# Gate and up projections by seven block products for eight (one Strassen level) in an eight-core FFN and mixer kernel

## The chip, the cores and the metric

The kernel runs on all 8 cores of one Trainium2 chip (two dies: cores 0 to 3 and 4 to 7). Each core does the same work on its own 2192 tokens, with no traffic between cores. The metric is the device time of the slowest core in microseconds (us).

The same program took clearly longer in some of its executions, and in these some cores were granted a lower TensorE clock. Two numbers are given for most runs: the time of the fast runs, and the span on *clean* cores, those whose clock records hold no *reduced stretch*. This is a stretch in which the granted clock is down although TensorE is busy throughout (0.82 from 2278 to 2438 us in the run with x in fp16, core 5, by the view of stretches). In runs without a trace clean cores are picked by their mean clock. Spans are compared with spans: 2501 to 2502 us for the kernel before.

## The reference, cut to what matters

Two layers, each `x += 0.5*SwiGLU1(rms(x)); x += Mix(rms(x)); x += 0.5*SwiGLU2(rms(x))`. Width 1024, hidden width 2816 = 22 blocks of 128.

```python
def rmsnorm(x, g):
    xf = x.astype(jnp.float32)
    y = xf * lax.rsqrt(jnp.mean(xf * xf, axis=-1, keepdims=True) + EPS)
    return (y * g.astype(jnp.float32)).astype(x.dtype)

def swiglu(x, w_gu, w_down):
    gate, up = jnp.split(x @ w_gu, 2, axis=-1)
    return (jax.nn.silu(gate) * up) @ w_down
# ... mixer (RG-LRU and gated linear attention), states, final norm: unchanged by the change
```

## The kernel before

Everything is transposed: channels on partitions, tokens along columns. The activations `x` stay in SBUF as fp32 (70 KB per partition). The FFN runs in four calls, each in two halves of the tokens; a half has three tiles of 272 or 384 tokens, and beside it another half's mixer runs as independent work for the same engines. The kernel contains a list scheduler: it fixes, before anything runs, the order of the instructions of each engine, from a table of durations and a list `PLAN` of one rule per 25 us. So where an instruction is not ready its engine waits at it: after the change TensorE once stood for 7.0 us before a normed tile (`xn` L497 in the list of waits below). TensorE's results go to PSUM, eight banks in this program; a *hand-over* below means that the program lets TensorE write a bank again only when another engine has read it.

```python
TILES = [(0, 272), (272, 384), (656, 384), (1040, 384), (1424, 384), (1808, 384)]
HALVES = [[0, 1, 2], [3, 4, 5]]
NGU, NDN, NPG = 6, 5, 6        # slots: gate/up weights, down weights, pages of mixer weights
NF, NB = 10, 7                 # fp32 and bf16 buffers of the mixers
xn = sb("xn", [128, 3, KC, NMAX], F16)          # normed x of three tiles
# ... for a block j of 128 hidden channels and one tile (K = 1024 = 8 matmuls each):
P.op("pe", [mm(G, w.ap[:, kc*128:(kc+1)*128], xn[:, sl, kc, o0:o0+n], n, kc == 0, kc == KC-1) for kc in range(KC)], ...)
P.op("pe", [mm(U, w.ap[:, 1024+kc*128:1024+(kc+1)*128], xn[:, sl, kc, o0:o0+n], n, ...) for kc in range(KC)], ...)
act(sg[:, b, :n], lambda: bk(G)[:, :n], AF.Silu, ...)                        # ScalarE
tt(hb[:, hs_, jj, :n], lambda: bk(U)[:, :n], sg[:, b, :n], ALU.mult, ...)    # VectorE
# ... down projection of a group of j, for 8 blocks mc of output channels:
stt(x[:, mc, s:s+n], lambda: bk(v)[:, :n], 0.5, x[:, mc, s:s+n], ALU.mult, ALU.add, ...)   # VectorE: x += 0.5*psum
```

## Time and profile before

The median of the 3 fast runs was 2504.52 us (2504.2 to 2505.18); a fourth run was slow, 2987.9 us. The first lines come from the page of the profile: busy time by engine, four rows of the strip (40 slices, tenths busy; `PEclk` is the granted clock), the chain of work that ended last, and the four groups of the FFN (busy us, mean ns | idle before, and what ended it).

```profile
PE 2475.8 (99%) x16678; PEld 1543.5 (62%) x16678; DVE 1521.1 (61%) x3196; ACT 1327.3 (53%) x2560; POOL 625.4 (25%) x990
...
PE   7999999999999999999999999999999999999998
DVE  5545765657766568543644467665676666776346
ACT  3322678686767586311311149686848686753115
PEclk9999999999999999999999999999999999999999
...
PE 94%; ACT 3%; DVE 1%; DMA 1%; issue 0%; POOL 0%; DVEq 0%; ACTq 0%; POOLq 0%
...
L483 PE MATMUL ps<-xn,rgu 128*128 128x384 f16 (+2 forms) x8176 | 1317.3, 317 | 1.4 <-ACT sg L464 1.0
...
L470 DVE SCALAR_TENSOR_TENSOR x<-ps,x 128x384 f32<-128x384 f32 (+3 forms) x1192 | 599.8, 527 | 221.6 <-PE ps L483 190.0
L464 ACT ACTIVATE sg<-ps 128x384 f32<-128x384 f32 (+3 forms) x535 | 247.6, 470 | 833.8 <-PE ps L483 682.0
...
L476 DVE TENSOR_TENSOR hb<-ps,sg 128x384 f16<-128x384 f32 (+3 forms) x535 | 278.1, 528 | 413.7 <-PE ps L483 366.9
```

TensorE hardly waits; VectorE and ScalarE wait for it. The same from the other side is the list of TensorE's waits (what it waited for, total us, times, longest), some 20 us in all; these are its largest:

```profile
PE ps L483 <- DVE sqf L476: 9.8, 6, 7.7
PE ps L483 <- ACT sqf L464: 4.5, 4, 2.4
PE ps L483 <- ACT Bb L464: 1.7, 5, 0.5
```

`sqf` are squares for a norm. And by stretches (columns: window, then busy us and instruction counts of PE, weight loads, DVE, ACT, POOL; the last three numbers are clock, DMA share, GB/s): the first is beside a mixer, the second is FFN alone.

```profile
400.00:600.00 200.00, 199.87 (x1306) 117.12 (x1304) 125.07 (x246) 144.56 (x264) 47.16 (x78) 1.00 0.66 100
1100.00:1300.00 200.00, 200.00 (x1318) 128.77 (x1316) 100.67 (x200) 38.15 (x71) 26.91 (x45) 1.00 0.44 74
```

### The profile page before, as it was taken

Reading aid. Unit: us, or ns where it says so; the run is one execution under the profiler, and the core shown is the slowest. Engines: PE = TensorE matmul, PEld = TensorE weight load, DVE = VectorE, ACT = ScalarE, POOL = GpSimd, SP = SyncE. Lnnn points to the kernel's source line nnn. Section 1 sums busy time; section 2 is a strip of 40 time slices with the busy share of each in tenths; the row PEclk is TensorE's granted clock in tenths of the full one; section 3 lists DMA queues with packets and bytes.
Section 4 is the critical chain, followed back from the end, with each engine's and each line's share of the span. In section 5 each row is a group of like instructions: output and inputs, shape, how many; then the busy total and the mean of one; then the engine's idle time right before and its main releaser. Section 6 shows DMA issues by size and latency. Waiting matters only on the chain.

```text
span 2502.3 us, 47184 instructions; the slowest of 8 cores (2501.0 to 2502.3 us)
## 1 busy us (share of the span) xinstructions
PE 2475.8 (99%) x16678; PEld 1543.5 (62%) x16678; DVE 1521.1 (61%) x3196; ACT 1327.3 (53%) x2560; POOL 625.4 (25%) x990
## 2 busy tenths in 40 slices
PE   7999999999999999999999999999999999999998
PEld 4666665555666666666666666655566666666666
DVE  5545765657766568543644467665676666776346
ACT  3322678686767586311311149686848686753115
POOL 2222232313221314310201042313132314142102
PEclk9999999999999999999999999999999999999999
DMA  9656677666776779544444357676767667986412
GB/s 185 121 106 99 109 119 108 104 103 94 107 112 106 120 129 157 94 77 71 78 72 68 52 83 109 95 120 88 123 98 113 108 105 105 165 138 140 68 26 77
DMA packets 118049, 259.68 MB, mean 104 GB/s; under 512 B 12896, under 2 KB 23264, under 8 KB 117824
## 3 DMA queue, kind: packets, MB, share of 16 engines
q0 software_dynamic: 104576, 238.48, 60.6%
q1 hardware_dynamic: 12528, 17.59, 2.1%
q8 instruction: 144, 2.36, 0.4%
q14 instruction: 81, 0.66, 0.1%
q10 hardware_dynamic: 720, 0.59, 0.1%
HBM read 472.41 MB, written 13.65 MB: 194 GB/s over the span
## 4 chain that ended last, share of the span: by engine, by line
PE 94%; ACT 3%; DVE 1%; DMA 1%; issue 0%; POOL 0%; DVEq 0%; ACTq 0%; POOLq 0%
PE ps L483 93%; DMA x<-xT 1%; PE ps L482 1%; ACT Fb L464 1%; ACT L941 0%; ACT Fb L933 0%; DVE x L470 0%; DVE Fb L470 0%; ACT Fb L941 0%; PE ps L1128 0%; ACT Fb L942 0%; ACT sg L464 0%; ACT Bb L464 0%; ACT L464 0%; POOL x L492 0%
## 5 line engine op out<-in xcount | busy, mean ns | idle before, releaser
L483 PE MATMUL ps<-xn,rgu 128*128 128x384 f16 (+2 forms) x8176 | 1317.3, 317 | 1.4 <-ACT sg L464 1.0
L483 PEld LDWEIGHTS ps<-xn,rgu 128*128 128x128 f16 x8176 | 794.3, 98 | 458.9 <-issue 5.9
L470 DVE SCALAR_TENSOR_TENSOR x<-ps,x 128x384 f32<-128x384 f32 (+3 forms) x1192 | 599.8, 527 | 221.6 <-PE ps L483 190.0
L464 ACT ACTIVATE sg<-ps 128x384 f32<-128x384 f32 (+3 forms) x535 | 247.6, 470 | 833.8 <-PE ps L483 682.0
L483 PE MATMUL ps<-hb,rdn 128*128 128x384 f16 (+2 forms) x4008 | 678.9, 317 | 0.6 <-issue 0.3
L476 DVE TENSOR_TENSOR hb<-ps,sg 128x384 f16<-128x384 f32 (+3 forms) x535 | 278.1, 528 | 413.7 <-PE ps L483 366.9
L483 PEld LDWEIGHTS ps<-hb,rdn 128*128 128x128 f16 x4008 | 388.2, 98 | 224.9 <-issue 4.1
L541 POOL DMA_DIRECT2D rpg<-wmx x336 | 180.2, 539 | 725.9 <-PE ps L483 664.4
L483 PE MATMUL ps<-xnt,rpg 128*128 128x384 bf16 (+2 forms) x1536 | 262.0, 318 | 0.7 <-ACT Fb L464 0.4
L527 POOL DMA_DIRECT2D rgu<-wgu x168 | 90.5, 539 | 650.5 <-PE ps L483 648.5
L483 PEld LDWEIGHTS ps<-xnt,rpg 128*128 128x128 bf16 x1536 | 146.5, 98 | 90.2 <-issue 4.9
L464 ACT ACT_TABLE_LOAD x148 | 189.9, 1283 | 23.0 <-PE ps L483 19.1
L464 ACT ACTIVATE sqf<-x 128x384 bf16<-128x384 f32 (+2 forms) x220 | 102.7, 502 | 124.6 <-DVE x L476 64.2
L534 POOL DMA_DIRECT2D rdn<-wdn x166 | 88.4, 544 | 287.3 <-PE ps L483 285.0
L470 DVE SCALAR_TENSOR_TENSOR Fb<-Fb,cols_sb 128x384 f32<-128x384 f32 (+3 forms) x216 | 120.0, 565 | 59.9 <-ACT Fb L464 31.7
L464 ACT ACTIVATE Fb<-ps 128x384 f32<-128x384 f32 (+4 forms) x262 | 111.9, 465 | 36.6 <-PE ps L483 32.7
L470 DVE SCALAR_TENSOR_TENSOR Fb<-Fb 128x384 f32<-128x384 f32 (+2 forms) x144 | 88.6, 617 | 68.1 <-ACT Fb L933 53.7
L483 PE MATMUL ps<-mixin,rpg 128*128 128x384 bf16 (+2 forms) x768 | 124.8, 318 | 0.2 <-DVE mixin L470 0.2
L470 DVE SCALAR_TENSOR_TENSOR xn<-x,cols_sb,ps 128x384 f16<-128x384 f32 (+2 forms) x192 | 102.2, 586 | 12.2 <-ACT ps L606 12.1
L483 PEld LDWEIGHTS ps<-mixin,rpg 128*128 128x128 bf16 x768 | 74.8, 98 | 44.4 <-issue 1.2
L575 POOL TENSOR_TENSOR rsf<-rsf,sqf 128x384 f32<-128x384 f32 (+2 forms) x104 | 90.6, 885 | 18.5 <-ACT sqf L464 17.8
L476 DVE TENSOR_TENSOR x<-ps,x 128x384 f32<-128x384 f32 (+2 forms) x96 | 49.1, 530 | 42.4 <-PE ps L483 42.3
(136 smaller groups left out, 1766.0 us busy)
## 6 DMA issues: line engine op xcount, KB each, us to landing
rgu<-wgu POOLq DMA_DIRECT2D x168, 512.0 KB, 7.4
rpg<-wmx POOLq DMA_DIRECT2D x336, 256.0 KB, 6.4
rdn<-wdn POOLq DMA_DIRECT2D x166, 256.0 KB, 7.4
x<-xT POOLq DMA_DIRECT2D x10, 768.0 KB, 8.1
yT<-Fb SPq DMA_DIRECT2D x32, 192.0 KB, 2.9
rpg<-wgu POOLq DMA_DIRECT2D x7, 512.0 KB, 9.6
S0f<-S SPq DMA_DIRECT2D x12, 256.0 KB, 7.6
Sos<-S0f SPq DMA_DIRECT2D x12, 256.0 KB, 7.4
```

What stands on the lines that cost most here:

```text
L464: P.op("act", lambda h: h.activation(out=o_(), in_=i_(), func=func, scale=scale, **kw), reads, writes, dur=ac(n, ptr, 0 if callable(in_) e ...
L470: P.op("dve", lambda h: h.scalar_tensor_tensor(out=o_(), in0=a_(), scalar=scalar, in1=b_(), op0=op0, op1=op1), reads, writes, dur=dv(n, 0 ...
L476: P.op("dve", lambda h: h.tensor_tensor(out=o_(), in0=a_(), in1=b_(), op=op), reads, writes, dur=dv(n), prio=prio, port=not (callable(in0) ...
L482: return lambda h: h.matmul(o_(), lhsT=lhsT, rhs=rhs, start=start, stop=stop, skip_group_check=True)
L483: return lambda h: h.matmul(o_(), lhsT=lhsT, rhs=rhs, start=start, stop=stop)
L527: P.op("pool", lambda h: h.dma_start(out=s.ap.rearrange("p (a b) -> p a b", a=2), in_=wgu_d[fi, j].rearrange("p (a b) -> p a b", a=2)), wr ...
L534: P.op("pool", lambda h: h.dma_start(out=s.ap, in_=wdn_d[fi, j]), writes=s.keys, dur=600, sem=s.sem, nbytes=128 * 1024 * 4, prio=prio)
L541: P.op("pool", lambda h: h.dma_start(out=rpg[:, s, :], in_=wmx_d[l, k]), reads=[("go", 5, min(pg_n[0] // 3, 2))], writes=[("pg", s)], dur= ...
L575: P.op("pool", lambda h: h.tensor_tensor(out=out, in0=a, in1=b, op=ALU.add), reads, writes, dur=pl(self.n), prio=0, port=True)
```

## The change

Take the weights of block `j` as a 2 x 2 block matrix A (rows up and gate, columns the two halves of K) and two tiles of tokens as a 2 x 2 block matrix B (rows the two halves of K, columns the tiles). The four products of gate and up for two tiles are A times B: eight block products. Winograd's form of Strassen's method needs seven, at the price of sums of blocks of A and B beforehand, and of results afterwards. The intent is to take an eighth of the gate and up matmuls off TensorE, the only engine that is full, and to put the sums on the engines that have room. The diff, cut to its core:

```diff
+FT = [(0, 260), (260, 260), (520, 260), (780, 260), (1040, 288), (1328, 288), (1616, 288), (1904, 288)]
+PAIRS = [[(0, 1), (2, 3)], [(4, 5), (6, 7)]]
-NGU, NDN, NPG = 6, 5, 6
-NF, NB = 10, 7
+NGU, NGS, NDN, NPG = 3, 2, 5, 5
+NF, NB = 8, 6
+NST = 1
+SUMS = ("dve", "dve", "pool", "dve")
 ...
-        xn = sb("xn", [128, 3, KC, NMAX], F16)
+        xn = sb("xn", [128, 2, 7, 4, NP], F16)        # two pairs, 4 blocks of B and 3 sums each
+        gus = sb("gus", [128, NGS, 3, 512], F16)       # sums of weight blocks
 ...
+        def sums(w):                                   # once per j and half
+            for eng, out, a, b, op, ... in (
+                    (SUMS[0], g.ap[:, 0], A21, A22, ALU.add, ...),
+                    (SUMS[1], g.ap[:, 1], g.ap[:, 0], A11, ALU.subtract, ...),
+                    (SUMS[2], A21, A11, A21, ALU.subtract, ...),          # overwrites A21
+                    (SUMS[3], g.ap[:, 2], A12, g.ap[:, 1], ALU.subtract, ...)):
+                P.op(eng, lambda h, ...: h.tensor_tensor(out=out, in0=a, in1=b, op=op), ...)
 ...   # ffn_norm: as before for the two tiles of a pair, and then four sums of blocks of xn on VectorE
+            for out, a, b in ((4, 3, 1), (1, 1, 0), (5, 4, 0), (6, 2, 5)):
+                P.op("dve", lambda h, ...: h.tensor_tensor(out=B(out), in0=B(a), in1=B(b), op=op), ...)
 ...   # one j and one pair: 7 products of 4 matmuls into three PSUM banks X, Y, Z
+                prod(X, w.ap[:, 0], w.keys[0], 0, True, marks)
+                p1 = copy(X)                            # ScalarE, PSUM to qf
+                prod(Y, w.ap[:, 1], w.keys[1], 2, True)
+                add(Y, p1, u1)                          # VectorE, PSUM + qf
+                prod(Z, g.ap[:, 0], g.keys[0], 1, True)
+                p5 = copy(Z)
+                prod(X, g.ap[:, 1], g.keys[1], 5, False)    # accumulates on P1
+                u2 = copy(X)
+                prod(Z, g.ap[:, 2], g.keys[2], 3, False)
+                add(Z, u2, u2_)
+                prod(X, w.ap[:, 2], w.keys[2], 4, False)
+                add(X, p5, p5)
+                act(s2[0], p5[0], AF.Silu, ...)
+                ...tensor_tensor(out=hb[:, hs_, 1, :n], in0=u2_[0], in1=s2[0], op=ALU.mult)
+                prod(X, w.ap[:, 3], w.keys[3], 6, False)
+                act(s1[0], lambda: bk(X)[:, :n], AF.Silu, ...)
+                ...tensor_tensor(out=hb[:, hs_, 0, :n], in0=u1[0], in1=s1[0], op=ALU.mult)
 ...   # squares of a norm are added in one serial chain on GpSimd (two chains before); new PLAN
```

The sums need room, and SBUF was full: hence fewer weight slots, pages and mixer buffers.

## The prediction

> **What bounds it now.** TensorE. The page has it busy 99% of 2502.3 us, and 94% of the chain of work that ended last is PE. The granted clock is 0.999 on all cores. Start-to-start distances of consecutive matmuls in the trace are 163 ns at 384 columns, 116 at 272, 109 at 256: columns/2.4 plus about 2.7 ns. [...] Against that line the whole run loses only some 6 us beyond the fixed cost per matmul, apart from the start: the first matmul stream follows about 38 us of loads and norm. So nearly every matmul removed shows up as time, if the others keep up.
>
> **What the change removes.** Gate and up are 8448 matmuls over 3.08 M columns: 1284 us + 8448 x 2.7 ns = 1306 us. Seven products of 4 matmuls for each weight block and tile pair are 9856 matmuls over 2.70 M columns (tiles of 260 and 288, 252 in the last layer): 1123 + 27 = 1150 us. Removed: 156 us of PE. Added to PE: eight tiles for six in the down projection, 1408 more matmuls x 2.7 ns = 4 us. LDWEIGHTS (98 ns, overlapped) stays below the 111 ns of a 260-column matmul. PE floor: about 2352 us.
>
> **What it adds elsewhere** (352 weight-block/tile-pair steps; distances of back-to-back instructions: VectorE 348 ns at 272 columns, ScalarE 277).
> - VectorE: three PSUM adds for two multiplies, 1056 x 0.35 = +370 us, less about 235 for the old multiplies; 704 16-bit multiplies, about 0.2 each: +145; 528 weight sums of 512, about 0.33 each: +175; norm block sums +43; smaller tiles +40. [...] Busy goes from 1521 to about 2060 us, 61% to 85-88%.
> - ScalarE: three copies and two SiLU for two SiLU, about +320 us: 53% to about 70%. In the two mixer stretches (300-1000 and 1500-2200 us), where it is 70-80% busy already by the windows view, about 90%.
> - GpSimd: 176 sums x 1.15 us, about +200 us: 25% to 36%.
> - DMA bytes unchanged; gate/up slots fall from 6 to 3, pages 6 to 5.
>
> **How much lies on the critical path.** The PE saving wholly. The additions are meant to hide, but slack shrinks: one PSUM bank takes P1, is copied, then accumulates three more products with an eviction between each[...], so PE must find other work each time. I estimate 25-30 us of new PE waits, mostly beside the mixers, plus 5 us at the start (two tiles and weight sums needed sooner) and 2 us at the tail.
>
> **Predicted:** 2385 us (-4.8%), 8 in 10 between 2352 and 2450. Faster by over 2%: 0.88; within 2%: 0.10; slower: 0.02.
>
> **What would show it right.** Gate/up matmuls 9856, 111 and 123 ns apart; PE busy about 97-98% of a shorter span; idle time before PE released by VectorE or ScalarE, tens of us in total, in the mixer stretches; VectorE 80-90%; ScalarE near 70%. FFN-only stretches (formerly 1000-1500 us) shrink by nearly 10%, mixer stretches by less.
>
> **What would make it wrong.** VectorE saturating (16-bit sums not at double rate[...]), so that the FFN runs at VectorE's pace: over 2450. A lower granted clock with sums as operands. Weight loads late with three slots. A schedule so good that hardly any wait appears: 2352-2360.

Four passages are cut from this text, where it is marked. 2352 us and the 25-30, 5 and 2 us of waits make about 2385. The trace before has no plain 16-bit sum, so the 0.2 and 0.33 us for 16-bit instructions had no measurement behind them when they were written. The trace after the change has them (start to start, medians): 204 ns at 260 columns and 219 at 288 for the multiplies, 334 to 336 at 512 for the weight sums of VectorE, and 1112 for those of GpSimd; the 64 block sums take 50.8 us in all. Weight loads take 98 ns on the page before and 98 to 99 on the page after. What a copy with its hand-over costs TensorE was not shown before the change; in the trace after it, four chains in which ScalarE waited for the product and TensorE for the copy took 0.56 to 0.64 us from the end of a product to the next matmul.

## The result, and the profile after

The kernel after is correct and slower. Its fast runs take 2628.5 us, two slow runs 2901.57 and 2943.19 us (die 0 at a clock of 0.82 to 0.85, die 1 undisturbed at 2623 to 2628 us). The ratio of the fast runs is 1.049 (95% interval 1.047 to 1.052). Ratios in this text are the mean time of one kernel's fast runs over that of the other's of the same rounds, so not quite the ratio of the medians. In the fast state the cores span 2622 to 2627 us (2623 to 2627 in the profiled run).

The same lines of the page after the change:

```profile
PE 2410.1 (92%) x19374; PEld 1801.8 (69%) x19374; DVE 2141.1 (82%) x5461; ACT 1699.8 (65%) x3853; POOL 868.1 (33%) x1240
...
PE   5999999999899998899899979999989999979997
DVE  6878887878887879877977788777898877889777
ACT  3454786877786869543443459697779686866344
PEclk8999999999999999899999989999999999989998
...
PE 57%; ACT 20%; DVE 17%; issue 3%; POOL 1%; DMA 1%; POOLq 0%; DVEq 0%; ACTq 0%; SPq 0%
...
L509 PE MATMUL ps<-xn,rgu 128*128 128x288 f16 (+2 forms) x5504 | 812.6, 283 | 57.0 <-DVE xn L497 21.0
...
L509 PE MATMUL ps<-xn,gus 128*128 128x288 f16 (+2 forms) x4224 | 631.3, 284 | 57.8 <-DVE xn L664 33.8
...
L491 ACT ACTIVATE qf<-ps 128x288 f32<-128x288 f32 (+2 forms) x1056 | 395.2, 396 | 291.4 <-PE ps L509 225.5
...
L503 DVE TENSOR_TENSOR ef<-ps,qf 128x288 f16<-128x288 f32 (+2 forms) x704 | 301.3, 436 | 83.1 <-PE ps L509 61.3
```

TensorE is now idle for 8% of a longer span, and the chain that ended last runs over ScalarE and VectorE for 37% of the span. TensorE's largest waits:

```profile
PE ps L509 <- DVE xn L664: 34.0, 13, 6.1
PE ps L509 <- ACT qf L491: 30.6, 45, 2.1
PE ps L509 <- DVE xn L497: 21.0, 9, 7.0
PE ps L510 <- DVE x L497: 20.7, 25, 4.0
PE ps L510 <- DVE sqf L503: 13.1, 12, 6.6
PE ps L510 <- DVE xnt L497: 12.2, 6, 4.1
PE ps L509 <- DVE qf L503: 11.8, 18, 1.4
```

`xn` L664 are the sums of activation blocks, `xn` L497 the normed tiles, `qf` the copies of the seven-product form, `x` the evictions of the down projection. By stretches: beside a mixer, at a change between FFN halves, and FFN alone.

```profile
450.00:600.00 150.00, 143.02 (x1077) 97.10 (x1076) 119.35 (x275) 120.36 (x256) 48.39 (x71) 1.00 0.73 103
1000.00:1100.00 100.00, 78.42 (x620) 55.91 (x618) 87.87 (x223) 76.53 (x180) 57.09 (x82) 0.90 0.69 111
1350.00:1500.00 150.00, 150.00 (x1227) 119.72 (x1225) 114.44 (x302) 55.60 (x138) 31.31 (x42) 1.00 0.50 72
```

In this stretch inside a half, where the FFN is alone, nothing is lost: TensorE is busy for all 150 us although VectorE works 76% of the time. At the change between halves TensorE is idle for a fifth of the time, and the granted clock falls to 0.90.

**A ledger of TensorE time.** I took every distance from the start of one matmul to the start of the next and split it into an ideal part, columns/2.4 + 2.7 ns (the line through the distances of the trace before: 163 ns at 384 columns, 116 at 272, 109 at 256; for other than full 128 x 128 matmuls at most the distance itself), time lost to a lower clock, and idle time. In this sum (mine, from the trace records):

| us | before | after | difference |
|---|---|---|---|
| matmuls | 16678 | 19374 | |
| ideal | 2436.2 | 2283.6 | -152.6 |
| idle between matmuls | 51.8 | 292.9 | +241.1 |
| lost to a lower clock in matmuls | 0 | 33.5 | +33.5 |

How the loss divides between the last two rows depends a little on the method (a second reckoning gave 288 and 39 us for 293 and 34). The three differences sum to +122.0 us; core 2's span grew by 125.8 us, from 2501.1 to 2626.9.

The saving is there to the microsecond. It was spent, and 122 us more, on waits and on the lower clock.

**What the idle time waits for.** For each gap of more than 60 ns before a matmul I took, among the instructions whose result or buffer this matmul needs, the one that ended last in the trace, and grouped the gaps (the total differs a little from the ledger's, since here gaps are counted against planned durations; core 2):

| idle us, by what ended last | sum | norms for the FFN and the final norm | FFN copies, adds, SiLU, multiplies | evictions of down | mixer | other |
|---|---|---|---|---|---|---|
| before | 34.6 | 11.7 | 2.1 | 0.6 | 13.6 | 6.6 |
| after | 308.2 | 100.6 | 90.1 | 32.1 | 62.1 | 23.1 |

So a third of the new idle time is at norms, a third in hand-overs of PSUM banks and the other FFN work inside the seven products, and the rest beside the mixers and in the down projection. As a check, the same gaps put down to what the profile alone says ended them give 97 us at norms after the change and 9 before.

### The profile page after: what moved, and what is told of

It is laid out like the page before. It is cut to its first block, busy times and chain, and to the rows that moved or that the text cites. A ratio compares the mean times of both kernels' runs of the same rounds, so it can differ in the third digit from the quotient of the medians.

```text
span 2626.9 us, 58244 instructions; the slowest of 8 cores (2623.0 to 2626.9 us)
## 1 busy us (share of the span) xinstructions
PE 2410.1 (92%) x19374; PEld 1801.8 (69%) x19374; DVE 2141.1 (82%) x5461; ACT 1699.8 (65%) x3853; POOL 868.1 (33%) x1240
## 4 chain that ended last, share of the span: by engine, by line
PE 57%; ACT 20%; DVE 17%; issue 3%; POOL 1%; DMA 1%; POOLq 0%; DVEq 0%; ACTq 0%; SPq 0%
PE ps L509 29%; PE ps L510 28%; DVE x L497 3%; DVE Fb L497 2%; ACT Fb L491 2%; ACT qf L491 2%; ACT L491 2%; DVE gus L579 2%; DVE xn L497 2%; ACT ef L491 2%; ACT L979 1%; DVE ef L503 1%; ACT Fb L971 1%; DVE xnt L497 1%; ACT Bb L491 1%
## 5 line engine op out<-in xcount | busy, mean ns | idle before, releaser
L509 PE MATMUL ps<-xn,rgu 128*128 128x288 f16 (+2 forms) x5504 | 812.6, 283 | 57.0 <-DVE xn L497 21.0
L510 PE MATMUL ps<-hb,rdn 128*128 128x288 f16 (+3 forms) x5528 | 759.5, 282 | 19.7 <-DVE x L497 14.4
L497 DVE SCALAR_TENSOR_TENSOR x<-ps,x 128x288 f32<-128x288 f32 (+2 forms) x1544 | 633.3, 435 | 84.0 <-PE ps L510 75.4
L509 PE MATMUL ps<-xn,gus 128*128 128x288 f16 (+2 forms) x4224 | 631.3, 284 | 57.8 <-DVE xn L664 33.8
L509 PEld LDWEIGHTS ps<-xn,rgu 128*128 128x128 f16 x5504 | 530.4, 98 | 201.6 <-issue 87.8
L491 ACT ACTIVATE qf<-ps 128x288 f32<-128x288 f32 (+2 forms) x1056 | 395.2, 396 | 291.4 <-PE ps L509 225.5
L509 PEld LDWEIGHTS ps<-xn,gus 128*128 128x128 f16 x4224 | 407.8, 99 | 166.9 <-issue 82.6
L579 POOL TENSOR_TENSOR rgu<-rgu 128x512 f16<-128x512 f16 x172 | 211.8, 1231 | 490.5 <-DVE gus L579 466.9
L503 DVE TENSOR_TENSOR ef<-ps,qf 128x288 f16<-128x288 f32 (+2 forms) x704 | 301.3, 436 | 83.1 <-PE ps L509 61.3
L503 DVE TENSOR_TENSOR qf<-ps,qf 128x288 f32<-128x288 f32 (+2 forms) x352 | 153.8, 437 | 56.3 <-PE ps L509 42.3
```

The costliest lines, as they stand in the source:

```text
L491: P.op("act", lambda h: h.activation(out=o_(), in_=i_(), func=func, scale=scale, **kw), reads, writes, dur=ac(n, ptr, 0 if callable(in_) e ...
L497: P.op("dve", lambda h: h.scalar_tensor_tensor(out=o_(), in0=a_(), scalar=scalar, in1=b_(), op0=op0, op1=op1), reads, writes, dur=dv(n, 0 ...
L503: P.op("dve", lambda h: h.tensor_tensor(out=o_(), in0=a_(), in1=b_(), op=op), reads, writes, dur=dv(n), prio=prio, port=not (callable(in0) ...
L509: return lambda h: h.matmul(o_(), lhsT=lhsT, rhs=rhs, start=start, stop=stop, skip_group_check=True)
L510: return lambda h: h.matmul(o_(), lhsT=lhsT, rhs=rhs, start=start, stop=stop)
L579: P.op(eng, lambda h, out=out, a=a, b=b, op=op: h.tensor_tensor(out=out, in0=a, in1=b, op=op), reads, [wr], dur=dv2(512) if eng == "dve" e ...
```

## The experiments

The theories to tell apart:

1. *Load*: the added work on VectorE, ScalarE and GpSimd, by its duration, makes TensorE wait.
2. *Order and hand-overs*: the fixed order, with more dependences per matmul, makes TensorE wait even where the other engines have time.
3. *Frame*: not the seven products but what came with them costs: tile pairs, norms per pair, buffers given up.
4. *Contention*: GpSimd's sums slow VectorE down.

In the first six runs the order of instructions stays as it is in the kernel after; only some instructions work on 8 columns for their full width, so results are wrong. The buffers they leave unwritten are set to zero at the start, which delays the first matmul: it starts at 6.6 us after the change, at 11.5 us in the third of these runs and at 16.3 us in the sixth.

### One weight sum on GpSimd made short

```diff
-  ...tensor_tensor(out=out, in0=a, in1=b, op=op)
+  m = 8 if eng == "pool" else 512
+  ...tensor_tensor(out=out[:, :m], in0=a[:, :m], in1=b[:, :m], op=op)
```

> Same order of instructions as the changed kernel (2628 us); only the one weight sum per block that GpSimd makes is done on 8 columns instead of 512 (wrong result on purpose). GpSimd loses about 190 us of busy time. Theory P ([...]VectorE instructions with two SBUF operands are stretched by 114 us in total in the changed kernel against 25 us in the kernel before, and that reaches TensorE): stretched VectorE time falls by more than half, VectorE busy falls by 60 us or more without losing an instruction, time falls by 30 to 60 us, to 2570-2600. Rival Q (the order of instructions and the dependences set the time, not the contention): under 10 us, 2618-2628.

All runs were disturbed (2675.8 to 2937.4 us). In one of them die 0 was clean by its mean clock: 2595.9 to 2598.9 us, some 28 us under the 2623 to 2627 us of the kernel after; single cores of two other runs agree (2592 to 2600 us). This fits with the trace of the kernel after. These are its three weight sums on VectorE, all of 512 columns, in the groups view by shape:

```profile
L579 DVE TENSOR_TENSOR gus<-gus,rgu 128x512 f16<-128x512 f16 x172 | 95.7, 556 | 1.8
L579 DVE TENSOR_TENSOR gus<-rgu,gus 128x512 f16<-128x512 f16 x172 | 85.2, 495 | 1.7 <-PE ps L509 0.9
...
L579 DVE TENSOR_TENSOR gus<-rgu 128x512 f16<-128x512 f16 x172 | 73.1, 425 | 10.5 <-PE ps L509 6.5 <-DMA rgu<-wgu 3.6
```

The same work takes 425, 556 and 495 ns on average. The GpSimd sum overwrites `A21`, so it may start as soon as VectorE's first sum has read it, which is just when VectorE starts the second. Over all weight sums on VectorE, the 398 that overlap no two-operand GpSimd instruction last 417 ns (nine in ten under 425, none over 800); the 130 that overlap one last 722 ns on average, 41 of them over 800 (1316 ns in the mean of these; a GpSimd sum lasts 1231). VectorE's instructions that read PSUM were not stretched: at 288 columns the evictions into x take 450 ns with a two-operand GpSimd instruction beside them and 452 without, the adds of the seven products 452 and 451. What makes VectorE slower beside GpSimd is not shown; that its sums take longer is. With the GpSimd sum made short, the trace of this run (core 7) has the same three sums at 423 to 439 ns, and VectorE busy for 2098 us where it was 2141; the text had expected 60 us less or more. Contention is thus real, and one part of the loss; without a fast run its size of some 28 us rests on one die and four single cores, and it includes what the shorter sum saves by itself.

### All four weight sums made short

```diff
-  ...tensor_tensor(out=out, in0=a, in1=b, op=op)
+  ...tensor_tensor(out=out[:, :8], in0=a[:, :8], in1=b[:, :8], op=op)
```

> Same order as the changed kernel; all four weight sums per block (three on VectorE, one on GpSimd) on 8 columns (wrong result on purpose). VectorE loses about 140 us of planned work and the stretch. P: 2550-2580. Q (TensorE waits because of the order and the dependences, not of VectorE's load): 2610 or more.

Median 2609.5 us, ratio 1.045; clean cores 2584 to 2588 us, some 39 us less, between the two ranges above. Idle time on core 0 is 258 us for 293. Against the run above, three more sums on VectorE are worth only another 10 us.

### All added VectorE work made short

```diff
 # besides the weight sums, all on 8 columns:
+  ...tensor_tensor(out=B(out)[:, 0, :8], in0=B(a)[:, 0, :8], in1=B(b)[:, 0, :8], op=op)      # block sums
+  tt(out[0][:, :8], lambda: bk(v)[:, :8], c[0][:, :8], ALU.add, ...)                          # PSUM adds
+  ...tensor_tensor(out=hb[:, hs_, 1, :8], in0=u2_[0][:, :8], in1=s2[0][:, :8], op=ALU.mult)   # multiplies
```

> Same order; weight sums, sums of activation blocks, the three PSUM adds and the 16-bit multiplies all on 8 columns (wrong result on purpose): nearly all the VectorE and GpSimd work that the change adds is gone, VectorE busy falls from 82% to near 55%. If VectorE's load alone made the 240 us of new TensorE waits, the time falls to 2400 or less. If the order in which instructions were planned around that load, and the dependences, hold most of it, it stays near 2520 (my estimate from following the dependences with the trace's durations: 2522).

Median 2559.0 us, ratio 1.022; all cores 2551 to 2558 us, -70 us. VectorE is busy 63%, about as much as before the change (61%), and TensorE's idle time is still 226 us. So the added load of VectorE, with GpSimd's sums, acting by its durations in a fixed order, is 67 us of the 241.

### The three ScalarE copies made short

```diff
-  act(o, lambda: bk(v)[:, :n], AF.Copy, n, [v], [k], prio=0)
+  act(o[:, :8], lambda: bk(v)[:, :8], AF.Copy, n, [v], [k], prio=0)
```

> Same order; the three ScalarE copies out of PSUM per step on 8 columns (wrong result on purpose): ScalarE loses about 240 us of busy time, and the hand-over P1 - copy - next product in the same PSUM bank is 0.2 us shorter each time. Theory S (ScalarE and that hand-over matter): 30 us or more faster. Rival: under 10 us, 2618-2628.

The runs had stretches at lower clock (2643 to 2874 us, ratio 1.057 by the two that count as fast). In the profiled run, a slow one, two cores had no reduced stretch: 2609.2 and 2598.9 us, 16 and 28 us less than the same cores after the change, the second with 267 us of idle time. This lies between the two ranges above. The gaps that a copy ended fall from 46 to 22 us. The copies are a cost, not the cost.

### The norms' products and block sums made short

```diff
-  stt(xn[:, pi, b, kc % 4, :n], x[:, kc, s:s + n], ..., lambda v=v: bk(v)[:, :n], ...)
+  stt(xn[:, pi, b, kc % 4, :8], x[:, kc, s:s + 8], ..., lambda v=v: bk(v)[:, :8], ...)
 # and the four block sums as above
```

> Unchanged order; the eight VectorE products of each FFN norm and the four sums of activation blocks on 8 columns (wrong result on purpose). In the changed kernel's trace about 80 us of TensorE's waits end at a norm of the next half or its block sums. Theory B (at the boundaries between FFN halves the longer norm chain is exposed): 40 us or more faster on undisturbed cores, to 2585 or less, and the waits on the norm's products nearly gone. Rival (the instructions' own time is not it; the norm comes late because the VectorE queue in front of it is full): under 25 us.

Median 2600.1 us, ratio 1.038; cores 2587 to 2599 us, -28 to -38 us: more than the rival allowed and less than theory B asked for. Idle time at norms falls from 101 to 72 us. Even with VectorE's part nearly gone, squares, sums and the root still stand between two halves.

### All FFN work of VectorE, ScalarE and GpSimd made short

```diff
 # weight sums, norm products, block sums, copies, adds, SiLU, multiplies, and
-  stt(x[:, mc, s:s + n], lambda v=v: bk(v)[:, :n], 0.5, x[:, mc, s:s + n], ...)
+  stt(x[:, mc, s:s + 8], lambda v=v: bk(v)[:, :8], 0.5, x[:, mc, s:s + 8], ...)
```

> Unchanged order; all FFN work of VectorE, ScalarE and GpSimd on 8 columns: sums, block sums, adds, multiplies, copies, SiLU, norm products, evictions of the down projection (wrong result on purpose). If engine work made the waits, TensorE's idle time falls from 293 us to near the 53 us of the kernel before and the time to about 2350. If the order and the hand-overs (TensorE - engine - TensorE on one PSUM bank) hold them, it stays at 2490-2530 (estimate from following the dependences: 2500).

Median 2500.0 us, ratio 0.9985; cores 2489 to 2498 us. This is the main result of the first group. The busy times on the page of this run:

```profile
PE 2360.2 (94%) x19374; PEld 1812.1 (73%) x19374; DVE 1169.8 (47%) x5467; ACT 1342.9 (54%) x3853; POOL 686.4 (27%) x1240
```

With nearly all FFN work off the other engines, the seven-product order only reaches the time of the kernel before, although its matmuls are 153 us shorter (some 10 us of its time is the later start). 169 us of idle time remain where there were 52: 62 us at norms, 56 at the mixers, 27 at hand-overs. About half of the new idle time (124 of 241 us) is thus the duration of that work, and the other half comes with the order, which was planned around that work, and with the mixers. The pure load theory, by durations in a fixed order, falls.

**Five runs with the order planned anew, and one in the default order.** A shorter instruction in an old order cannot show what a planner would make of it. For the next runs I changed three lines of the scheduler, so that the rule in force follows the progress of the whole schedule, and searched for new rules. All of them but the run in the default order, and the later runs, have this edit:

```diff
+        cur = [0]
-            return plan[min(int(t / window), len(plan) - 1)]
+            return plan[min(cur[0], len(plan) - 1)]
+            cur[0] = max(cur[0], int(bt / window))
```

For the unchanged kernel after, this search found no better plan than its own (a planned length, which is how long the planner itself reckons the schedule to be, of 2549 us against 2548), so that was not run.

### Eight ordinary products in the new frame

```diff
-  ...seven products...
+  for t in range(2):
+      G, U = VT("G"), VT("G")
+      # 8 matmuls each from the same weight slot and the same pair slot; SiLU and multiply as before the change
+  # no weight sums, no block sums
```

> Correct result. The changed kernel's frame kept (pairs of tiles of 260 and 288, its buffers: 3 gate/up slots, 8 and 6 work buffers, two pair slots for the normed activations), but eight ordinary products and no sums; order planned anew. If the seven products and their added work are the loss, and the frame costs nothing, this is 2504-2520. If the frame itself costs (fewer buffers, two pair slots instead of three tile slots), it is 2560-2590, as its plan of 2563 says.

Correct. Median 2642.5 us, ratio 1.056. Most cores had reduced stretches; in the cores view two of them have none (core, span, granted clock):

```profile
core 1: 2638.0 us, clock 0.965
core 2: 2583.7 us, clock 0.988
core 3: 2587.4 us, clock 0.989
core 4: 2638.5 us, clock 0.965
```

So the frame *alone*, with no sums at all, costs about 83 us against the kernel before, on clean cores. The ledger of core 2 is 2448 ideal, 101 idle, 13 clock: 12 us of the 83 are the fixed cost of more and smaller matmuls (20782 for 16678), 49 are idle time, 13 clock, and most of the rest comes after the last matmul starts (15 us for 5). The largest waits on this core:

```profile
PE ps L514 <- DVE xn L501: 21.6, 8, 5.0
PE ps L514 <- DVE sqf L507: 13.2, 11, 6.3
PE ps L514 <- ACT sqf L495: 12.3, 15, 4.1
```

All three are norms. In the grouping used above: 64.5 us at norms (11.7 before), 16.6 at mixers, 4.2 at hand-overs, 3.4 at down. With eight products the rest is nearly as it was before the change; it is the norm of the next half that is no longer hidden.

### Added VectorE work made short, order planned anew

The edit is that of the third run, with the short durations in the planner's table too.

> As the run with all added vector work on 8 columns (wrong result on purpose), but the order planned anew for those short instructions. That run kept the order that had been made around the load and came to 2559. If VectorE's load acts through the order that it forces, this falls to 2465-2500 (the plan is 2459). If the order has nothing to do with it, it stays near 2555.

Fast runs 2530.5 and 2531.8 us, ratio 1.011; cores 2517 to 2529 us. That missed the text above on the slow side. The same work in the old order took 2551 to 2558 us, which agrees with a cost of VectorE's load through the order too: the planner had to place work around a full VectorE. TensorE idle is 189 us here, 226 in the old order.

### x held in fp16, and the room spent on buffers

```diff
-NGU, NGS, NDN, NPG = 3, 2, 5, 5 ; NF, NB = 8, 6 ; NST = 1 ; SUMS = ("dve", "dve", "pool", "dve")
+NGU, NGS, NDN, NPG = 4, 2, 5, 6 ; NF, NB = 10, 7 ; NST = 2 ; SUMS = ("dve", "dve", "dve", "dve")
-  x = sb("x", [128, KC, T], F32)
+  x = sb("x", [128, KC, T], F16)
-  xn = sb("xn", [128, 2, 7, 4, NP], F16)
+  xn = sb("xn", [128, 3, 7, 4, NP], F16)      # a third pair slot
```

> The residual stream x kept in fp16 instead of fp32, which frees 35 KB per partition: a third pair slot for the normed activations, work buffers back to 10 and 7, pages to 6, two state buffers; sums on VectorE alone; order planned anew (plan 2472). Result correct within fp16 rounding of x, if the tolerance allows it. Theory F (SBUF that the seven-product form takes away is a main part of the loss): 2480-2520. Rival: within 20 us of the same kernel with fp32 x and the small buffers.

Correct, and the fastest correct form with seven products. The runs counted as fast took 2553 to 2576 us (ratio 1.025, interval 1.019 to 1.031), above the text; but each had most cores at a lower mean clock, in the profiled one by a reduced stretch of about 160 us on every core (granted clock 0.82 from 2278 to 2438 us on core 5). Clean cores in other runs took 2522 to 2530 us. Against 2623 to 2627 us that is about 100 us, without taking one sum away. It still is 20 to 29 us over the kernel before. Idle time is 195 us.

### All weight sums on VectorE

```diff
-SUMS = ("dve", "dve", "pool", "dve")
+SUMS = ("dve", "dve", "dve", "dve")
```

> Correct result. All four weight sums on VectorE, none on GpSimd, and the order planned anew for that. Contention theory P: [...]VectorE's stretch falls from 114 us to 50 or less, and the run ends within 50 us of the length that the kernel's own scheduler plans (2528), where the changed kernel ends 80 us over its plan of 2548: 2550-2585. If contention is not it, VectorE's extra 60 us of work shows and the run is 2620 or more.

Correct. 2627 to 2963 us, every run disturbed. In the profiled run every core had a reduced stretch; the best, at 2597 to 2598 us, had one of 159 us, which at the clock of 0.82 of the run with x in fp16 took some 29 us (159 x 0.18), so about 2568 us undisturbed is an estimate; idle time 238 us. In two other runs two cores each took 2575 to 2580 us at a mean clock of 0.975 to 0.976, within the range that the text gave to contention and some 47 us under the kernel after. Moving the sum to the busier engine and planning anew helps, in agreement with the contention; 20 us of it the planner had already reckoned (2528 us for 2548), so the two are not separated.

### The order by the default rule

```diff
+        code = 0      # in policy(): every rule of PLAN is the neutral one
```

> Correct result. The changed kernel with its scheduler's default rules instead of the tuned list of rules per 25 us window; every instruction is the same, only the order differs. If order is a large lever here, it is 80 us or more slower than 2628 (plans: 2643 against 2548). If the engines' work alone set the time, within 20 us.

Correct. 2739 to 2794 us (the longest a slow run), ratio 1.098; clean cores 2701 to 2706 us, so 78 us or so over the same work in its searched order, with 355 us of idle time. The order is worth as much as the added VectorE work (70 us in the third run).

### Short VectorE work, x in fp16, planned anew

This joins two of the runs above, as a bound: free VectorE work and buffers as before.

> Both at once: x in fp16 with the larger buffers, and the added vector work on 8 columns (wrong result on purpose), order planned anew. A bound on what the seven products could give if neither the vector work nor SBUF were short: the plan is 2410, I expect 2415-2450. If it is not below 2480, a further cause is missing from my list.

2468.9 us, ratio 0.986 (0.984 to 0.988); cores 2463 to 2467 us. It is slower than the narrower range above, but shows that the seven products do gain, 36 us, where VectorE does not have to do the work and the buffers are there. Against the same buffers with the VectorE work (2522 to 2530 us), the short work takes off another 60 us. 144 us idle still remain.

**Four runs on the frame.** Was the frame's cost the memory given up, the tile pairs, or only a weak search of mine?

### The kernel before, planned anew

> The kernel before, its order only planned anew by the search and the scheduler edit that the re-planned runs used. If that search is as good as the one the kernel came with: 2498 to 2515 us (its own plan is 2497 us long against 2495 us). If my search is what made the eight products in the new frame slow: 2540 us or more.

Correct, 2509.8 us, ratio 1.002 (1.0004 to 1.004); cores 2507 to 2508 us. For this kernel my search is as good as its own to 0.2%, which speaks against the 83 us of the frame being an artefact of it. It does not exclude it: the search for the frame was another one, and its list still holds 27 of the 103 rules made for the seven products.

### The kernel before with three gate/up slots

```diff
-NGU, NDN, NPG = 6, 5, 6
+NGU, NDN, NPG = 3, 5, 6
```

> The kernel before with three gate/up weight slots for six, re-planned; nothing of the seven products. Displaced-memory theory: 2580 to 2620 us (plan 2580 us). Tile-pairs theory, in which the slots are harmless: 2498 to 2520 us.

2570.8 us, ratio 1.026. The result was wrong, as far as the code shows because the kernel's list of early loads assumes nine early slots, and with six a block is overwritten before it is read. This also delays the start: 48 of its 116 us of idle time lie in the first 100 us, against 12 of 55 in the kernel before planned anew. The later part remains comparable, as the amount and shape of the work are the same: 68 us against 43. Three slots cost about 25 us of idle time there, a good deal less than the text above had for them.

### The kernel before with fewer mixer buffers

```diff
-NGU, NDN, NPG = 6, 5, 6
-NF, NB = 10, 7
+NGU, NDN, NPG = 6, 5, 5
+NF, NB = 8, 6
```

> The kernel before with five pages for six and 8 and 6 activation buffers for 10 and 7, re-planned; gate/up slots stay at six. Displaced-memory theory: 2555 to 2590 us (plan 2554 us). Tile-pairs theory: 2498 to 2520 us.

2565.8 us, ratio 1.023, clean cores 2547 to 2549 us, and wrong in the same way. The time lies in the range that the displaced-memory theory gave, but for another reason: the whole excess is in the delayed start, since eight early slots also fall short of nine loads. After the first 100 us its idle time is 39 us, that of the kernel before planned anew 43. For the old kernel these buffers are harmless after the start, against my expectation.

### Seven products with the mixers' buffers back

```diff
-NGU, NGS, NDN, NPG = 3, 2, 5, 5 ; NF, NB = 8, 6 ; NST = 1 ; x in F32
+NGU, NGS, NDN, NPG = 3, 2, 5, 6 ; NF, NB = 10, 7 ; NST = 2 ; x in F16 (pays for it)
```

> The seven-product kernel with x held in fp16, which pays for six pages, 10 and 7 activation buffers and two state buffers again; three gate/up slots and two pair slots as after the change, one weight sum on GpSimd; re-planned. Displaced-memory theory with the mixers' buffers as the larger part: 2550 to 2590 us (plan 2488 us, plus the clock and contention excess of 60 to 80 us that the other runs of this form showed), against 2628 us after the change. If only the third pair slot and the sums' engine made the fp16-x kernel of an earlier run faster: 2610 to 2640 us.

Correct. The fast runs, 2581 and 2590 us (ratio 1.032), had cores with reduced stretches (mean clock 0.964 to 0.967, against 0.976 to 0.980 on the clean cores); clean cores took 2554 to 2564 us, 60 to 70 us under the kernel after. Idle time is 230 us for 293. So buffers that the old kernel could spare (here with a second state buffer, which the run above did not test) are worth a good deal to the new one, mostly at hand-overs (90 to 55 us) and down (32 to 18 us); norms stay at 101 us. The planner had reckoned 60 us of this (2488 us for 2548). x in fp16 was not tried alone, but the traces leave the type little room: evictions of 288 columns into x take 450 ns for 452, normed products 504 for 508, squares 441 for 440.

The mended forms of the two wrong kernels, and eight products in the new frame with all buffers back, would have closed the question of the frame.

### The main runs in one table

| run | clean cores, us | idle | clock |
|---|---|---|---|
| before | 2501-2502 | 52 | 0 |
| before, planned anew | 2507-2508 | 55 | 2 |
| eight products in the new frame | 2584-2587 | 101 | 13 |
| after | 2623-2627 | 293 | 33 |
| after, default order | 2701-2706 | 355 | 46 |
| all added VectorE work short | 2551-2558 | 226 | 26 |
| the same, planned anew | 2517-2529 | 189 | 26 |
| all FFN work of the other engines short | 2489-2498 | 169 | 11 |
| mixers' buffers back (x fp16) | 2554-2564 | 230 | 27 |
| x fp16, buffers, third pair slot, sums on VectorE | 2522-2530 | 195 | 52, with a reduced stretch |
| the same buffers and VectorE work short | 2463-2467 | 144 | 16 |

## Why the prediction was right or wrong

The prediction was 2385 us, range 2352 to 2450, 88% for faster; the result is 2628 us, slower.

- *"So nearly every matmul removed shows up as time, if the others keep up."* The first half held: 16678 to 19374 matmuls, and their ideal time fell by 152.6 us, where the text had 156 less 4. The line columns/2.4 + 2.7 ns, read from the trace before, fits the trace after the change as well: 122 to 123 ns at 288 columns, 111 at 260, and 216 at 512 columns in both traces.
- *What it adds elsewhere.* Right in kind. VectorE 2141 us for 2060, ScalarE +373 us for +320, GpSimd +243 for +200. The 16-bit sums do run at twice the rate of adds from PSUM: start to start 334 ns for 512 columns, against 367 ns for 288 (0.65 against 1.27 ns a column). On VectorE what was short is mostly contention. By my count VectorE's instructions last 114 us longer than their uncontended durations would give, 25 us before the change.
- *"I estimate 25-30 us of new PE waits, mostly beside the mixers, plus 5 us at the start (two tiles and weight sums needed sooner) and 2 us at the tail."* **This is the step that failed.** The term measured 241 us of idle time and 33 us of lost clock. The start alone cost about 20 us for 5 (32 us of idle time between matmuls in the first 100 us, 12 before). The estimate was taken from one hand-over at a time: "TensorE must find other work each time". The runs show in its place:
  - 89 us more at norms. 53 of these come with the frame and need no Strassen form at all (64.5 us in the eight-product run). In that run each product needs its own tile alone; with seven products the second tile of the pair is needed from the third product on, and four of the seven need block sums of both tiles.
  - 88 us more at hand-overs and the other FFN work inside the seven products, which eight products in the same frame do not have (4 us).
  - 48 us more at the mixers, 31 in the down projection, 16 elsewhere. That the engines are too full to be on time fits with this, but no run shows it for these places alone.
  - 33 us of clock. After the gaps the clock records of core 2 show TensorE at half clock, in 17 stretches of one or more steps of 3.41 us each. The prediction had no term for this, and so none for what a wait costs beyond its length.
- *Where it sits.* "Mostly beside the mixers" was wrong: norms and hand-overs hold two thirds. "FFN-only stretches shrink by nearly 10%" was right in mechanism: from 1350 to 1500 us TensorE is busy throughout, at full clock. At the change between halves, from 1000 to 1100 us, it was idle for a fifth of the time.
- *What would make it wrong.* VectorE saturating was the named risk. Its time limit, over 2450 us, was passed, but not for this reason: FFN-only stretches kept TensorE's pace at 76% VectorE. The hold-up by GpSimd is real (722 ns for 417 above) and cost at most some 28 us (first experiment). The clock did not fall by the sums as operands: it was 1.00 in these stretches. Waits for weight loads are not among TensorE's larger waits (0.4 us in all on gate and up weights, 0.4 on down). So none of these three explains most of the loss. It lies in waits at single places, at norms and hand-overs, where an engine that is not full on average is late; VectorE's added work has a part in them, 67 us of idle time in a fixed order.

The planner inside the kernel after has a planned length of 2548 us, that of the kernel before 2495 us. So about 53 us of slowdown are in the planned order itself, before any contention or clock; the rest appears on the chip.

How the parts share the loss is only bounded, since they interact. Durations of all FFN work off TensorE, old and new, in a fixed order are 124 of the 241 us of idle time; the new frame is about 83 us of span by itself; buffers are 60 to 70 us for the seven-product form; planning anew around short VectorE work is 30 us; VectorE's added work with the buffers back is 60 us. These overlap and must not be summed. Open is what in the frame exposes the norms: the norms by pairs, the serial chain of their sums, the fewer slots, or tiles that no longer match those of the mixers.

## What to carry to other kernels

When the bound engine is 99% busy, taking work from it pays only if the order of all the rest survives: count the dependences and the on-chip memory that the new form takes, and not only the busy time it adds. Test the frame by itself first (the old arithmetic in the new tiles and buffers): here this one run would have shown about 80 us of cost before a line of the new method was written. Price a wait of the matmul engine above its length where the clock falls after it (here 33 us on 241 us of new idle time).

## What the traces showed besides

- Half clock, in the profiled run of the kernel after. All 17 half-clock stretches of core 2 start on one fixed grid of 3.41 us. The grid step before such a stretch was 0 to 36% busy (each matmul counted as columns/2.4 + 2.7 ns), and in 16 of the 17 no idle stretch inside that step was longer than 2.8 us, so these were not single long gaps. Apart from the first 30 us, every step under 36% busy was followed by half clock, and at full clock none over 38% was. On all eight cores the 129 steps before half clock were at most 39% busy, and those at full clock that stayed there at least 38%.
- Reduced clock. The kernel before is dense on all 8 cores, with random inputs, at a granted clock of 0.999 in its fast runs. In the slow runs of all kernels the mean clock of the slower die is 0.80 to 0.96, often alike for pairs of cores (0.915, 0.915, 0.925 and 0.925 on die 0 in the profiled run with the GpSimd sum short). Reduced stretches of about 160 us stand in the traces of the runs with x in fp16 (at 0.82) and with all weight sums on VectorE.
- VectorE beside GpSimd. 16-bit sums of 512 columns on VectorE that overlap a two-operand GpSimd instruction took 722 ns on average, those that do not 417 ns.
- What the seven-product form cost besides its matmuls: -153 us of matmul time, +241 us of waits, +33 us of clock.
